# Seven-product stage: the low parts of the first weight sum on VectorE, and pads that put the tiles on one place modulo 256 bytes

## The chip, the cores and the metric

The kernel runs on one core of a Trainium2 chip. The metric is the device time of one execution in microseconds; the median of several executions stands for a kernel. TensorE (PE in the profile; PEld is its weight load) multiplies, VectorE (DVE), ScalarE (ACT) and GpSimd (POOL) do the rest, and the queue of SyncE (SP) issues nearly all loads and stores.

## The reference

One decoder layer on x of 1024 tokens by 1024 channels in float32. Cut to what matters:

```python
h = rms_norm(x, norm_mix_pre)
z = h @ w_in                                   # 1024 x 7424
z_pool, z_q, z_rwkv, z_gate = split(z)
y_pool = pool_branch(z_pool, ...) @ w_proj_pool
y_mem  = mem_attention(z_q, mem_n, w_mem_kv) @ w_proj_mem
y_rwkv = rwkv_branch(...) @ w_proj_rwkv        # a recurrence over the tokens
merged = gates[0] * y_pool + gates[1] * y_rwkv + gates[2] * y_mem
x = x + rms_norm(merged @ w_o, norm_mix_post)
h = rms_norm(x, norm_ffn_pre)
u_gate, u_val = split(causal_dwconv(h @ w_ffn_up, conv_w, conv_b))   # 1024 x 5632
x = x + rms_norm((gelu(u_gate) * u_val) @ w_ffn_down, norm_ffn_post)
```

## The kernel before

All gemms multiply float32 as three products of shorter numbers. A number is split into a high part (a copy into the type float32r, by ScalarE) and a low part (the number minus its high part, a subtraction), and `mm3` (lines 167 to 169) issues three matmuls of 128 by 128 weights with 512 moving columns: high x high, high weights x low moving, low weights x high moving. In the profile these are the tile pairs psg<-hh,whi, psg<-hl,whi and psg<-hh,wlo.

The stages, in the order of time, with the moving tiles and the weights:

- the input projection, moving hh and hl, weights whi and wlo. The recurrence of the RWKV branch runs among its gemms (lines 528 to 709: short float32 matmuls on tiles such as HV, AR, BKN); 928 steps of `mm3`
- attention and pooling with their projections: moving oh, ol, ph and pl
- the merge (moving yh, yl) and the output projection (mgh, mgl)
- the first five pairs of blocks of the up projection (h2h, h2l), with weights whi and wlo
- the seven-product stage (`up_pair`, PSUM tiles psf): the other 17 pairs of blocks of the up projection. The two blocks of a pair, gate and value, are cut in halves a11, a12 and a21, a22 over the channels, and the pair is computed with seven products in place of eight (Strassen's scheme). The panels B11, B21, B22, T4 lie in h2h and h2l, T1 and T2 and T3 in tiles t. The weights of the products are, in this order: a11 with B11; the first sum a21 + a22 with T1; the second sum, first sum minus a11, with T2; a12 with B21; a11 - a21 with T3; the third sum, a12 minus second sum, with B22; a22 with T4. First and second sum are done by GpSimd (line 1012) in the same tile sm, the third by VectorE, also in sm. `parts` splits the weights: high parts by ScalarE (line 1026), low parts by GpSimd (line 1027), each in two halves of 128 x 256. A product is 4 steps of `mm3`, 12 matmuls; a pair is 84. ScalarE and VectorE take the products out of PSUM and combine them (lines 1056 to 1075: u, z), ScalarE begins the convolution (line 1043, d<-z,pv), VectorE adds its taps (line 1045)
- the down projection, also with seven products (PSUM tiles psd, moving f, weights u)

The order on each engine is set by the scheduler of the tile framework, which keeps the order of dependent instructions; the first sum of a pair is made about one pair ahead.

Weights of the seven products have six buffers in turn, `n = nwt[0] % 6`: for n < 2 a tile of the pool `ow`, otherwise two tiles of the pool `pmp`. These pools lie at different places. A place is here the first byte of a tile within a partition, modulo 256; all tiles that matter have rows of a multiple of 256 bytes. The built programs have these places:

| tiles | before | after |
| --- | --- | --- |
| hh, hl, h2h, h2l, yh, yl, mgl (moving) | 224 | 224 |
| whi, wlo, wraw, sm, the a of later pairs | 192 | 224 |
| mgh, oh, ol, ph, pl (moving) | 64 | 224 |
| T1 and T2 (moving) | 64 | 224 |
| T3 (moving) | 224 | 224 |
| weights of the seven products, pool ow | 64 | 224 |
| weights of the seven products, pool pmp | 224 | 224 |
| f and u of the down projection | 64 | 224 |
| tiles of the recurrence (HV, AR, BK, NT and others) | 64 | 224 |
| constants ones, ident, bonesr, cent | 192 | 192 |

Of the kernel before, what the change touches and what calls it, by code (L numbers as in the profile page):

```python
# [9 lines left out]
F32 = mybir.dt.float32  # L10
FR = mybir.dt.float32r
AF = mybir.ActivationFunctionType
ALU = mybir.AluOpType
# [4 lines left out]
P = 128  # L18
# [26 lines left out]
def trunk_kernel(ctx: ExitStack, tc: tile.TileContext, xT, memT, pvec, w_in, w_kv, w_upd, w_upg,  # L45
                 w_pool, w_ppool, w_pmem, w_prwkv, w_o, w_fup, w_fdn, out):
    nc = tc.nc
    V, A, G, PE, SP = nc.vector, nc.scalar, nc.gpsimd, nc.tensor, nc.sync

    const = ctx.enter_context(tc.tile_pool(name="const", bufs=1))  # L50
    wp = ctx.enter_context(tc.tile_pool(name="wp", bufs=1))
# [53 lines left out]
                        base=-1, channel_multiplier=-1)  # L105
    G.memset(smask, 1.0)
    G.memset(smask.rearrange("p (c s) -> p c s", s=C)[:, :, 0:1], 0.0)
    eps = const.tile([P, 3], F32, name="eps")
    for j, e in enumerate((NORM_EPS, L2_EPS, LNX_EPS)):
        G.memset(eps[:, j:j + 1], e)  # L110
# [112 lines left out]
    for k in range(KC):  # L223
        tag = ("X01", "X11", "HV", "HV")[k // 2]
# [76 lines left out]

    def shifted(m, dst):

        zc = wp.tile([P, 1], F32, name="zc", tag="zc", bufs=4)

        def evac(t0, ps):
            d = dst[:, t0:t0 + 512]
            A.activation(d, ps, AF.Identity, scale=omu[:, m:m + 1])
            if t0 == 0:
                V.tensor_copy(zc, ps[:, 511:512])  # L310
            else:
                V.scalar_tensor_tensor(d[:, 0:1], zc, col("mu", m), d[:, 0:1], op0=ALU.mult,
                                       op1=ALU.add)
            V.scalar_tensor_tensor(d[:, 1:512], ps[:, 0:511], col("mu", m), d[:, 1:512],  # L314
                                   op0=ALU.mult, op1=ALU.add)
        return evac
# [532 lines left out]
    for hd in range(4):  # L849
        for t0, _ in HALVES:  # L850
            s = slice(t0, t0 + 512)
            q = as_.tile([P, 512], F32, name="q", tag="q", bufs=2)
            SP.dma_start(q, d_zq[hd][:, s])
            qh = as_.tile([P, 512], FR, name="qh", tag="qh")
            ql = as_.tile([P, 512], FR, name="ql", tag="ql")
            split(q, qh, ql, V)
            po = pss.tile([P, 512], F32, name="po", tag="s")
            for u in range(2):
                ps = psg.tile([P, 2, 256], F32, name="psco", tag="g0")
                for tt in range(2):  # L860
                    ts_ = slice((2 * u + tt) * P, (2 * u + tt + 1) * P)
                    mm3(ps[:, tt], (qh[:, ts_], ql[:, ts_]), (kh[:, hd], kl[:, hd]), True, True)
                mx = as_.tile([P, 8], F32, name="mxs", tag="mxs", bufs=2)
                V.reduce_max(mx[:, 0:2], ps, axis=AX.X)
                V.tensor_scalar(mx[:, 2:4], mx[:, 0:2], -SC, None, op0=ALU.mult)
                pr = as_.tile([P, 2, 256], F32, name="prb", tag="prb", bufs=2)
                for tt in range(2):
                    act(pr[:, tt], ps[:, tt], AF.Exp, bias=mx[:, 2 + tt:3 + tt], scale=SC,
                        accum_out=mx[:, 4 + tt:5 + tt])
                V.reciprocal(mx[:, 6:8], mx[:, 4:6])  # L870
                V.tensor_tensor(pr, pr, mx[:, 6:8].unsqueeze(2).broadcast_to([P, 2, 256]), op=ALU.mult)
                pt = (psc if u else psk).tile([P, 2, 2, P], F32, name="ptr", tag="c" if u else "k")
                for tt in range(2):
                    for m in range(2):
                        PE.transpose(pt[:, m, tt], pr[:, tt, m * P:(m + 1) * P], ident)
                pth = as_.tile([P, 2, 256], FR, name="pth", tag="pth", bufs=2)
                ptl = as_.tile([P, 2, 256], FR, name="ptl", tag="ptl")
                split(pt.rearrange("p m t s -> p m (t s)"), pth, ptl, V)
                for m in range(2):
                    mm3(po[:, u * 256:(u + 1) * 256], (vh[:, hd, m], vl[:, hd, m]), (pth[:, m], ptl[:, m]),  # L880
                        m == 0, m == 1)
            split(po, oh[hd][:, s], ol[hd][:, s], V)
        pool_products(hd)
        if hd < 2:
            pool_sums(hd + 2)
        for j, ev in fill[2 * hd:2 * hd + 2]:
            in_block(j, ev, 1)
# [109 lines left out]
    def up_pair(i):  # L997
        c = i % 2

        def load(nm, tag, j, k0):  # L1000
            if i == EARLY:
                t = ow.tile([P, 4, P], F32, name=nm, tag="xt" if tag == "whi" else "ss", bufs=2)
                SP.dma_start(t, w_fup[j][:, k0:k0 + 4])
                return [t[:, :2], t[:, 2:]]
            t = [wp.tile([P, 2, P], F32, name=nm, tag=f"{tag}{c}", bufs=4) for _ in range(2)]
            for u in range(2):
                SP.dma_start(t[u], w_fup[j][:, k0 + 2 * u:k0 + 2 * u + 2])
            return t

        def both(eng, out_, a, b, op):  # L1010
            for u in range(2):
                eng.tensor_tensor(out_[u], a[u], b[u], op=op)  # L1012

        def parts(src):

            n = nwt[0] % 6
            nwt[0] += 1
            if n < 2:
                w = ow.tile([P, 2, 4, P], FR, name="wt", tag=f"q{n}")
                w = [w[:, 0], w[:, 1]]  # L1020
            else:
                w = [pmp.tile([P, 4, P], FR, name=f"wt{e}", tag=f"n{8 + (n + 1) % 4 + 4 * e}")
                     for e in range(2)]
            for u in range(2):
                us = slice(2 * u, 2 * u + 2)
                A.copy(w[0][:, us], src[u])  # L1026
                last_low[0] = G.tensor_tensor(w[1][:, us], src[u], w[0][:, us].bitcast(F32), op=ALU.subtract).ins  # L1027
            return w

        nb = [0]  # L1030

        def prod(src, panel):
            w = parts(src)
            pool, tag = ((psg, "g0"), (psg, "g1"), (pss, "s"), (psk, "k"), (psg, "g0"), (psg, "g1"),
                         (pss, "s"))[nb[0]]
            nb[0] += 1
            ps = pool.tile([P, 512], F32, name="psf", tag=tag)
            for k in range(4):
                mm3(ps, (w[0][:, k], w[1][:, k]), panel(k), k == 0, k == 3)
            return ps  # L1040

        def convolved(z, d, j):
            A.activation(d, z, AF.Identity, scale=col("cw2", j), bias=col("cb", j))  # L1043
            for n, cw in ((1, "cw1"), (2, "cw0")):
                V.scalar_tensor_tensor(d[:, n:], z[:, :T - n], col(cw, j), d[:, n:], op0=ALU.mult,  # L1045
                                       op1=ALU.add)

        a11 = load("a11", "whi", i, 0)
        a21 = load("a21", "wlo", NF + i, 0)
        a22 = load("a22", "wlo", NF + i, 4)  # L1050
        a12 = load("a12", "whi", i, 4)
        sm = [wp.tile([P, 2, P], F32, name="sm", tag=f"wraw{c}", bufs=3) for _ in range(2)]
        z1, z2 = (ow1.tile([P, T], F32, name=f"z{e}", tag=f"q{4 + 2 * e + c}") for e in range(2))
        c11, c12, c21, c22 = z1[:, :512], z1[:, 512:], z2[:, :512], z2[:, 512:]
        u2 = ow.tile([P, 512], F32, name="u2", tag="xt", bufs=2)
        A.copy(c11, prod(a11, B11))
        both(G, sm, a21, a22, ALU.add)
        A.copy(c22, prod(sm, T1))
        both(G, sm, sm, a11, ALU.subtract)
        V.tensor_tensor(u2, c11, prod(sm, T2), op=ALU.add)  # L1060
        V.tensor_tensor(c22, c22, u2, op=ALU.add)
        V.tensor_tensor(c11, c11, prod(a12, B21), op=ALU.add)
        both(V, a21, a11, a21, ALU.subtract)
        p7 = prod(a21, T3)
        third = V.tensor_tensor(c21, u2, p7, op=ALU.add).ins
        if i == NF - 1:
            down.extend(down_loads())
            down.append(third)
        both(V, sm, a12, sm, ALU.subtract)
        V.tensor_tensor(c12, c22, prod(sm, B22), op=ALU.add)  # L1070
        last_sum[0] = V.tensor_tensor(c22, c22, p7, op=ALU.add).ins
        d1, d2 = (ow.tile([P, T], F32, name=f"d{e}", tag=f"q{2 + e}") for e in range(2))
        convolved(z1, d1, i)
        act(d1, d1, AF.Gelu_apprx_tanh)
        V.tensor_tensor(c21, c21, prod(a22, T4), op=ALU.add)
        convolved(z2, d2, NF + i)
        V.tensor_tensor(d1, d1, d2, op=ALU.mult)
        (G if i == NF - 1 else SP).dma_start(d_f[i], d1)
# [530 lines left out]
```

## Time and profile before

| | us |
| --- | --- |
| median of 3 executions | 2084.89 (2083.38 to 2085.0) |
| profiled execution | 2084.65 |
| its span, first to last instruction | 2082.7 |
| PE busy | 2026.5 |
| DVE busy | 1358.2 |
| ACT busy | 1070.6 |
| POOL busy | 810.8 |

The profile shows one execution. "Busy" is the time in which an engine worked on an instruction; matmuls are pipelined and overlap, and their ends are modelled, so the interval between the starts of two matmuls says more than the duration of one. A row of the view in order of time gives start and duration in us, engine, line, operation, tiles (out<-in), shape and, in brackets, how long the engine was idle before and who ended that. A row of the view of waits gives who waited for whom, the total in us, the times and the longest.

### The profile page before, as it was taken

The page shows a single profiled execution, that of the slowest core. Times are in us where ns is not written, and L with a number is a line of the kernel's source. Part 1 is how long each engine was busy: PE and PEld are TensorE (multiplying, and loading weights), DVE is VectorE, ACT ScalarE, POOL GpSimd, SP SyncE. Part 2 cuts the span into 40 slices and gives each one's busy share as a digit, 9 for nine tenths or more (in the row PEclk, how much of TensorE's full clock was granted, in tenths as well). Part 3 has the DMA queues.
Part 4 walks back from the last instruction along what each step waited for, and adds up shares of the span by engine and source line. Part 5 has one row for each costly group of instructions (what it writes and reads, how often), then busy time and mean ns, then how long its engine had stood idle before and what let it go on. Part 6 is the DMA issues. An engine that isn't in the chain of part 4 may idle for free.

```text
span 2082.7 us, 34125 instructions
## 1 busy us (share of the span) xinstructions
PE 2026.5 (97%) x12246; PEld 1559.1 (75%) x12246; DVE 1358.2 (65%) x2167; ACT 1070.6 (51%) x2252; POOL 810.8 (39%) x917
## 2 busy tenths in 40 slices
PE   8999999999999999999999999998999999999997
PEld 5777767776778667876878878776778877777886
DVE  6567437664667357833795452769877777777798
ACT  7585348623772368434566243545443444444644
POOL 5521213121222121212122355565578888842341
PEclk9999999999999999999999999999999999999999
DMA  4312211120212021213526443634222222169766
GB/s 155 129 41 74 67 51 67 67 82 22 87 61 89 30 92 44 86 55 120 172 84 223 129 134 107 220 102 151 94 88 83 82 78 76 61 185 273 168 178 152
DMA packets 176713, 221.83 MB, mean 107 GB/s; under 512 B 16544, under 2 KB 128288, under 8 KB 176544
## 3 DMA queue, kind: packets, MB, share of 16 engines
q1 hardware_dynamic: 163616, 204.44, 30.2%
q0 software_dynamic: 11856, 14.16, 4.2%
q8 instruction: 97, 1.59, 0.3%
q10 hardware_dynamic: 1072, 1.05, 0.1%
q14 instruction: 72, 0.59, 0.1%
HBM read 170.30 MB, written 49.28 MB: 105 GB/s over the span
## 4 chain that ended last, share of the span: by engine, by line
PE 36%; DVE 5%; DMA 4%; POOL 3%; issue 2%; ACT 2%; SPq 1%; POOLq 0%; ACTq 0%; DVEq 0%
PE psg L167 6%; PE psg L169 6%; PE psg L168 6%; PE psf L169 3%; PE psf L167 3%; PE psf L168 3%; POOL wt L1027 2%; PE psd L168 2%; PE psd L169 2%; PE psd L167 2%; DMA R<-d_f 1%; POOL sm L1012 1%; DMA a<-in_w_fup 1%; ACT d L1043 1%; DMA fw<-in_w_fdn 1%
## 5 line engine op out<-in xcount | busy, mean ns | idle before, releaser
L131 POOL TENSOR_TENSOR wlo<-wraw,whi 128x256 fp32r<-128x256 f32 x472 | 410.4, 878 | 951.7 <-ACT whi L128 760.2
L167 PE MATMUL psg<-hh,whi 128*128 128x512 f32 x928 | 383.6, 413 | 2.5 <-DVE kv L314 2.5
L169 PE MATMUL psg<-hh,wlo 128*128 128x512 f32 x928 | 379.8, 409 | 0.1
L168 PE MATMUL psg<-hl,whi 128*128 128x512 f32 x928 | 378.8, 408 | 0.0
L128 ACT CAST whi<-wraw 128x256 fp32r<-128x256 f32 x472 | 182.7, 403 | 227.9 <-PE psg L168 122.1
L167 PEld LDWEIGHTS psg<-hh,whi 128*128 128x128 f32 x928 | 174.6, 188 | 46.5 <-DVE kv L314 3.8
L169 PEld LDWEIGHTS psg<-hh,wlo 128*128 128x128 f32 x928 | 174.3, 188 | 45.9 <-POOL wlo L131 5.1
L168 PEld LDWEIGHTS psg<-hl,whi 128*128 128x128 f32 x928 | 174.7, 188 | 42.9 <-issue 3.6
L1027 POOL TENSOR_TENSOR wt<-a,wt 128x256 fp32r<-128x256 f32 x136 | 133.8, 1012 | 30.8 <-ACT wt L1026 30.8
L167 PE MATMUL psd<-f,u 128*128 128x512 f32 x292 | 115.0, 394 | 5.7 <-ACT f L1347 3.4
L168 PE MATMUL psd<-f,u 128*128 128x512 f32 x292 | 115.0, 394 | 1.0 <-DVE f L1351 1.0
L169 PE MATMUL psd<-f,u 128*128 128x512 f32 x292 | 114.3, 393 | 0.4 <-DVE u L1351 0.4
L1027 POOL TENSOR_TENSOR wt<-sm,wt 128x256 fp32r<-128x256 f32 x102 | 106.8, 1067 | 14.6 <-ACT wt L1026 14.6
L169 PE MATMUL psf<-h2h,wt 128*128 128x512 f32 x272 | 108.0, 397 | 0.4 <-POOL wt L1027 0.3
L168 PE MATMUL psf<-h2l,wt 128*128 128x512 f32 x272 | 107.0, 393 | 0.0
L167 PE MATMUL psf<-h2h,wt 128*128 128x512 f32 x272 | 106.8, 393 | 0.0
L1026 ACT CAST wt<-sm 128x256 fp32r<-128x256 f32 x102 | 37.9, 404 | 128.2 <-POOL sm L1012 124.2
L1045 DVE SCALAR_TENSOR_TENSOR d<-z,pv,d 128x1023 f32<-128x1023 f32 x68 | 91.6, 1347 | 12.0 <-ACT d L1043 9.5
L169 PE MATMUL psf<-t,wt 128*128 128x512 f32 x204 | 81.3, 399 | 1.9 <-POOL wt L1027 1.9
L168 PE MATMUL psf<-t,wt 128*128 128x512 f32 x204 | 80.3, 394 | 0.0
L167 PE MATMUL psf<-t,wt 128*128 128x512 f32 x204 | 80.2, 393 | 0.0
L685 DVE TENSOR_TENSOR HV<-ph,Hd 64x128 f32<-64x128 f32 x112 | 32.3, 289 | 71.8 <-PE ph L639 47.7
(422 smaller groups left out, 4751.3 us busy)
## 6 DMA issues: line engine op xcount, KB each, us to landing
wraw<-in_w_in SPq DMA_DIRECT2D x240, 128.0 KB, 2.3
a<-in_w_fup SPq DMA_DIRECT2D x128, 128.0 KB, 2.4
d_zg<-st SPq DMA_DIRECT2D x48, 256.0 KB, 2.7
wraw<-in_w_fup SPq DMA_DIRECT2D x80, 128.0 KB, 2.4
fw<-in_w_fdn SPq DMA_DIRECT2D x33, 256.0 KB, 4.5
fraw<-d_f SPq DMA_DIRECT2D x33, 256.0 KB, 5.2
wraw<-in_w_prwkv SPq DMA_DIRECT2D x64, 128.0 KB, 2.4
wraw<-in_w_o SPq DMA_DIRECT2D x64, 128.0 KB, 2.5
```

What stands on the lines that cost most here:

```text
L128: last_whi[0] = A.copy(hi, src).ins
L131: (V if lo_on_dve[0] else G).tensor_tensor(lo, src, hi.bitcast(F32), op=ALU.subtract)
L167: first = PE.matmul(ps, wh, xh, start=start, stop=False)
L168: PE.matmul(ps, wh, xl, start=False, stop=False)
L169: last_mm[0] = PE.matmul(ps, wl, xh, start=False, stop=stop).ins
L685: ready = V.tensor_tensor(HV[q, :, c + 1, e], ph[q], Hd[q], op=ALU.add).ins
L1012: eng.tensor_tensor(out_[u], a[u], b[u], op=op)
L1026: A.copy(w[0][:, us], src[u])
L1027: last_low[0] = G.tensor_tensor(w[1][:, us], src[u], w[0][:, us].bitcast(F32), op=ALU.subtract).ins
L1043: A.activation(d, z, AF.Identity, scale=col("cw2", j), bias=col("cb", j))
L1045: V.scalar_tensor_tensor(d[:, n:], z[:, :T - n], col(cw, j), d[:, n:], op0=ALU.mult, op1=ALU.add)
```

## The change

Two things are done. The pads: a tile of 8 columns that nobody uses in the pool `const`, eight buffers of one column in place of four for zc, and 32 columns in place of 8 for mxs. Allocation is in steps of 32 bytes, so these move the tiles allocated behind them (table above). And `parts` takes the engine of the low parts as an argument; the product with T1 passes VectorE, so the low parts of the first sum (2 per pair, 34 in all) are done there. `last_low` keeps the last low part on GpSimd.

```diff
     G.memset(smask.rearrange("p (c s) -> p c s", s=C)[:, :, 0:1], 0.0)
+    const.tile([P, 8], F32, name="cpad")
...
-        zc = wp.tile([P, 1], F32, name="zc", tag="zc", bufs=4)
+        zc = wp.tile([P, 1], F32, name="zc", tag="zc", bufs=8)
...
-                mx = as_.tile([P, 8], F32, name="mxs", tag="mxs", bufs=2)
+                mx = as_.tile([P, 32], F32, name="mxs", tag="mxs", bufs=2)
...
-        def parts(src):
+        def parts(src, eng):
...
                 A.copy(w[0][:, us], src[u])
-                last_low[0] = G.tensor_tensor(w[1][:, us], src[u], w[0][:, us].bitcast(F32), op=ALU.subtract).ins
+                low = eng.tensor_tensor(w[1][:, us], src[u], w[0][:, us].bitcast(F32), op=ALU.subtract)
+                if eng is G:
+                    last_low[0] = low.ins
             return w
...
-        def prod(src, panel):
-            w = parts(src)
+        def prod(src, panel, eng=G):
+            w = parts(src, eng)
...
-        A.copy(c22, prod(sm, T1))
+        A.copy(c22, prod(sm, T1, V))
```

Where the low parts stand now is seen in the middle of the seven-product stage. Lines are up to three later in the changed kernel (1012 becomes 1013, 1027 becomes 1028, 1060 becomes 1063), and the numbers of tiles are one higher. GpSimd before: the first sum of one pair (sm_16855), then the low parts T1 of the pair before it (wt1_16703<-sm_16675), its second sum in the same tile, and its low parts T2:

```order
L1012 TENSOR_TENSOR sm_16855<-a21_16843,a22_16847 128x256
L1012 TENSOR_TENSOR sm_16856<-a21_16844,a22_16848 128x256
L1027 TENSOR_TENSOR wt1_16703<-sm_16675,wt0_16702 128x256
L1027 TENSOR_TENSOR wt1_16703<-sm_16676,wt0_16702 128x256
L1012 TENSOR_TENSOR sm_16675<-sm_16675,a11_16659 128x256
L1012 TENSOR_TENSOR sm_16676<-sm_16676,a11_16660 128x256
L1027 TENSOR_TENSOR wt1_16725<-sm_16675,wt0_16724 128x256
L1027 TENSOR_TENSOR wt1_16725<-sm_16676,wt0_16724 128x256
```

GpSimd at the same place now:

```order
L1013 TENSOR_TENSOR sm_16856<-a21_16844,a22_16848 128x256
L1013 TENSOR_TENSOR sm_16857<-a21_16845,a22_16849 128x256
L1013 TENSOR_TENSOR sm_16676<-sm_16676,a11_16660 128x256
L1013 TENSOR_TENSOR sm_16677<-sm_16677,a11_16661 128x256
L1028 TENSOR_TENSOR wt1_16726<-sm_16676,wt0_16725 128x256
L1028 TENSOR_TENSOR wt1_16726<-sm_16677,wt0_16725 128x256
```

The low parts T1 are gone, and the second sum, which overwrites the first, follows the first sum of the next pair at once; it has to wait for the low parts on the other engine. VectorE before, at the same place: the subtraction a11 - a21 of the later pair, u and z of an earlier one, the third sum, z:

```order
L1012 TENSOR_TENSOR a21_16843<-a11_16839,a21_16843 128x256
L1012 TENSOR_TENSOR a21_16844<-a11_16840,a21_16844 128x256
L1060 TENSOR_TENSOR u2_16500<-z0_16498,psf_16550 128x512
L1061 TENSOR_TENSOR z1_16499<-z1_16499,u2_16500 128x512
L1062 TENSOR_TENSOR z0_16498<-z0_16498,psf_16571 128x512
L1012 TENSOR_TENSOR sm_16675<-a12_16671,sm_16675 128x256
L1012 TENSOR_TENSOR sm_16676<-a12_16672,sm_16676 128x256
L1065 TENSOR_TENSOR z1_16499<-u2_16500,psf_16593 128x512
L1070 TENSOR_TENSOR z0_16498<-z1_16499,psf_16614 128x512
```

VectorE now:

```order
L1013 TENSOR_TENSOR a21_16844<-a11_16840,a21_16844 128x256
L1013 TENSOR_TENSOR a21_16845<-a11_16841,a21_16845 128x256
L1063 TENSOR_TENSOR u2_16501<-z0_16499,psf_16551 128x512
L1028 TENSOR_TENSOR wt1_16704<-sm_16676,wt0_16703 128x256
L1064 TENSOR_TENSOR z1_16500<-z1_16500,u2_16501 128x512
L1028 TENSOR_TENSOR wt1_16704<-sm_16677,wt0_16703 128x256
L1065 TENSOR_TENSOR z0_16499<-z0_16499,psf_16572 128x512
L1013 TENSOR_TENSOR sm_16676<-a12_16672,sm_16676 128x256
L1013 TENSOR_TENSOR sm_16677<-a12_16673,sm_16677 128x256
L1068 TENSOR_TENSOR z1_16500<-u2_16501,psf_16594 128x512
L1073 TENSOR_TENSOR z0_16499<-z1_16500,psf_16615 128x512
```

The two low parts stand behind u and behind the first z; the rest of VectorE's order is the same, and TensorE's order is unchanged.

## Prediction

> **What bounds the kernel now.** I read the page first, then who waited for whom, then the matmuls in order of time, and last the three other engines in one stretch of the seven-product stage.
>
> ```profile
> span 2082.7 us, 34125 instructions
> PE 2026.5 (97%) x12246; PEld 1559.1 (75%) x12246; DVE 1358.2 (65%) x2167; ACT 1070.6 (51%) x2252; POOL 810.8 (39%) x917
> ...
> PE psn L1096 <- DVE s L1091: 8.3, 1, 8.3
> PEld psf L169 <- POOL wt L1027: 10.6, 22, 0.8
> ```
>
> TensorE is busy for 97% of the span, and its longest single wait is 8.3 us. So time can come from two things: from a shorter interval between matmuls that follow each other without a wait, and from small waits such as the 22 on GpSimd's low parts in the seven-product stage. The column "us" of a matmul is modelled; the interval is the difference of two starts. I took the starts 24 matmuls apart in three stages without waits: the input projection, the output projection, the down projection.
>
> ```profile
> 424.83 0.40 PE L169 MATMUL psg<-hh,wlo 128*128 128x512 f32 x1
> ...
> 430.43 0.40 PE L169 MATMUL psg<-hh,wlo 128*128 128x512 f32 x1
> ...
> 1359.64 0.39 PE L167 MATMUL psg<-mgh,whi 128*128 128x512 f32 x1
> ...
> 1365.18 0.39 PE L167 MATMUL psg<-mgh,whi 128*128 128x512 f32 x1
> ...
> 1959.73 0.39 PE L168 MATMUL psd<-f,u 128*128 128x512 f32 x1
> ...
> 1965.17 0.39 PE L168 MATMUL psd<-f,u 128*128 128x512 f32 x1
> ```
>
> 24 matmuls of the same shape take 5.60 us (233.3 ns each) with hh at place 224 and the weights at 192; 5.54 us (230.8 ns) with mgh at 64 and the weights at 192; and 5.44 us (226.7 ns) with f and u both at 64. Three stages could differ for other reasons. The seven-product stage has the test inside itself, since its weight tiles rotate over two places while the panels stay. These rows are the first matmuls of products of 12 matmuls each:
>
> ```profile
> 1606.16 0.39 PE L167 MATMUL psf<-h2h,wt 128*128 128x512 f32 x1
> ...
> 1608.88 0.40 PE L167 MATMUL psf<-t,wt 128*128 128x512 f32 x1
> ...
> 1625.30 0.39 PE L167 MATMUL psf<-h2h,wt 128*128 128x512 f32 x1
> ...
> 1628.11 0.39 PE L167 MATMUL psf<-t,wt 128*128 128x512 f32 x1
> ...
> 1630.84 0.39 PE L167 MATMUL psf<-t,wt 128*128 128x512 f32 x1
> ...
> 1633.64 0.39 PE L167 MATMUL psf<-h2h,wt 128*128 128x512 f32 x1
> ```
>
> B11 from 1606.16 has panel and weights at 224: 2.72 us. B11 one pair later, from 1625.30, has the same panel at 224 and its weights at 64: 2.81 us. T1 from 1628.11 has both at 64: 2.73 us; T2 from 1630.84 has the panel at 64 and the weights at 224: 2.80 us. Equal places are fast whichever place it is, unequal ones cost some 7 ns a matmul. I take the place modulo 256 as the cause, and 226.7 ns as the price with equal places. By the Trainium skill, page "SBUF — State Buffer", section "Who interferes with whom", TensorE never waits for anyone and only the port pair of VectorE and GpSimd is contended; it speaks against any effect of places on TensorE, and the four products above differ from it by 0.07 to 0.09 us each.
>
> **The pads.** They put moving tiles and weights of all gemms on 224. How many matmuls that are:
>
> ```profile
> L168 PE MATMUL psg<-hl,whi x928: 388/396/795, 7.4 to 1101.5; 128*128 128x512 f32 x186
> ...
> L168 PE MATMUL psf<-h2l,wt x272: 387/393/401, 1508.7 to 1844.8; 128*128 128x512 f32 x136
> ...
> L168 PE MATMUL psg<-h2l,whi x160: 388/396/628, 1380.7 to 1507.8; 128*128 128x512 f32 x160
> ...
> L168 PE MATMUL psg<-yl,whi x128: 392/395/398, 1196.0 to 1334.6; 128*128 128x512 f32 x128
> ...
> L168 PE MATMUL psg<-mgl,whi x128: 389/392/796, 1240.8 to 1380.0; 128*128 128x512 f32 x128
> ```
>
> Line 168 is one of the three matmuls of each step, so each count stands for three times as many.
> - hh and hl: 2784 x 6.6 ns = 18.4 us if each gains. Many stand among the short products of the recurrence, where the interval isn't 0.23 us:
>
> ```profile
> 252.03 0.39 PE L167 MATMUL psg<-hh,whi 128*128 128x512 f32 x1
> 252.35 0.45 PE L639 MATMUL ph<-HV,BKN 128*64 128x64 f32 x8
> ```
>
> Here it is 0.32 us, and nothing in the trace says that this one shrinks. I take two thirds, 12.2 us; ends 9 and 18.4.
> - h2h and h2l: 480 x 6.6 = 3.2 us. yh and yl, at the places of hh: 384 x 6.6 = 2.5 us. mgh and mgl: 384 x (230.8 - 226.7) = 1.6 us. The attention and pooling projections, 64 against 192 like mgh, are 2 x 8 blocks x 2 halves x 4 steps x 3 = 384: 1.6 us.
> - The down projection is at equal places already: 0. The seven-product stage is counted by itself below.
>
> Together 21.1 us. The extra buffers of zc and the wider mxs add no instruction: 0. The operands of copies, sums and activations change their places too. Those engines end few of TensorE's waits outside the seven-product stage (the 8.3 us above are the longest), so I count 0.
>
> **The low parts of the first sum.** 34 subtractions leave GpSimd and join VectorE. The stage is a loop of GpSimd, VectorE and ScalarE, which TensorE runs ahead of and then has to wait for. One round of it, the three engines one after the other (GpSimd, VectorE, ScalarE):
>
> ```profile
> 1664.78 0.73 POOL L1012 TENSOR_TENSOR sm<-a,a 128x256 f32<-128x256 f32 x1
> 1666.10 0.73 POOL L1012 TENSOR_TENSOR sm<-a,a 128x256 f32<-128x256 f32 x1 [0.58 <-DMA a<-in_w_fup]
> 1666.79 1.62 POOL L1027 TENSOR_TENSOR wt<-sm,wt 128x256 fp32r<-128x256 f32 x2
> 1668.36 1.90 POOL L1012 TENSOR_TENSOR sm<-sm,a 128x256 f32<-128x256 f32 x2
> 1670.21 1.42 POOL L1027 TENSOR_TENSOR wt<-sm,wt 128x256 fp32r<-128x256 f32 x2
> ...
> 1675.65 3.34 POOL L1027 TENSOR_TENSOR wt<-sm,wt 128x256 fp32r<-128x256 f32 x2 [0.84 <-ACT wt L1026]
> 1680.40 4.66 POOL L1027 TENSOR_TENSOR wt<-a,wt 128x256 fp32r<-128x256 f32 x4 [1.41 <-ACT wt L1026]
> 1685.02 0.74 POOL L1012 TENSOR_TENSOR sm<-a,a 128x256 f32<-128x256 f32 x1
> ...
> 1665.55 0.42 DVE L1012 TENSOR_TENSOR a<-a,a 128x256 f32<-128x256 f32 x1 [2.71 <-POOL sm L1012]
> 1666.87 0.94 DVE L1012 TENSOR_TENSOR a<-a,a 128x256 f32<-128x256 f32 x1 [0.89 <-POOL sm L1012]
> 1667.73 0.68 DVE L1060 TENSOR_TENSOR u<-z,psf 128x512 f32<-128x512 f32 x1
> 1668.51 1.15 DVE L1061 TENSOR_TENSOR z<-z,u 128x512 f32<-128x512 f32 x1
> ...
> 1670.98 1.82 DVE L1012 TENSOR_TENSOR sm<-a,sm 128x256 f32<-128x256 f32 x2 [0.72 <-POOL wt L1027]
> ...
> 1673.32 0.68 DVE L1070 TENSOR_TENSOR z<-z,psf 128x512 f32<-128x512 f32 x1
> ...
> 1674.03 1.25 ACT L1043 ACTIVATE d<-z,pv 128x1024 f32<-128x1024 f32 x1 [2.11 <-DVE z L1070]
> ```
>
> First sum to first sum is 20.24 us, while TensorE needs 19.14 for a pair (1606.16 to 1625.30). The loop is this: second half of the first sum (1666.10); low parts T1, second sum, low parts T2 on GpSimd; VectorE's third sum, which waited 0.72 us for GpSimd (1670.98); z (1673.32); ScalarE's convolution (1674.03); its casts, for which GpSimd waits 0.84 and 1.41 us; the last low parts, and so the load that the next first sum waits for. The stage confirms it: 16 rounds of 20.24 and a last pair of 19.1 make 342.9 us; it takes 336.7 (1508.4 to 1845.1: the quoted row's ends, out by the two matmuls around them); TensorE's lead, eaten up over the first seven pairs, is the other 6.2.
>
> Now the second sum has to wait until VectorE has read the first. By durations: the first sum's second half ends at 2.05 us of the round, as now. VectorE then does its subtraction, 2.09 to 2.52 (0.42 as at 1665.55, with GpSimd now idle there), u until 3.12 (0.68), and the first low part until 3.47. GpSimd's second sum may start at 3.5; it started at 3.58. Its first half is held up by z (0.67 to 1.15 us), ends at 4.7, and holds up VectorE's second low part until some 5.0 (0.95 as in the blocked rows). The second half of the second sum ends at 5.8 where it ended at 5.5 (1668.36 + 1.90 - 1664.78), and everything behind it, T2, third sum, z, convolution, moves by 0.3. So taking 1.6 us off GpSimd doesn't shorten the round: its work there lies beside VectorE's, and the 0.72 us that VectorE waited become 0.8 us of work and the rest a later start. Ends: 0.72 us shorter, if both low parts fit where VectorE waits now and nothing blocks; 1.2 longer, if both take 0.95 and only 0.72 of it is covered (2 x 0.95 - 0.72). I take 0.3, from the chain above.
>
> The stage: 16 x 20.54 + 19.1 - 6.2 = 341.5, so 4.8 us longer, and the faster matmuls gain nothing here, as TensorE only uses up its lead earlier.
>
> **The sum.** 21.1 - 4.8 = 16.3 us. The profiled execution took 2084.65 us (span 2082.7 and 1.95 around it), 0.24 under the median of 2084.89. 2084.65 - 16.3 = 2068.4.
>
> **The rivals.**
> - The loop gets shorter, not longer. At 0.72 us less it is 19.5, and less still where GpSimd's free time also shortens VectorE's blocked operations (0.94 to 0.42); TensorE's lead then lasts and it sets the stage: 17 x 84 x 226.7 ns = 323.7, and 0.6 of waits: 12.4 us less than 336.7. Time 2084.65 - 21.1 - 12.4 = 2051. For it: GpSimd is the busiest of the helpers in the stage. Against: the waits of 0.84 and 1.41 us on ScalarE, which it doesn't touch.
> - The loop is 1.2 us longer: 16 x 1.2 = 19.2, time 2082.8. VectorE's 0.94 and 1.82 show how often its operations are blocked; against it, GpSimd is idle when the first low part runs.
> - Places don't set the interval, and the four products differ by something else that rotates with the tiles. This is the side that ends slower: the pads bring 0, the move still costs 4.8, time 2089.5. It decides when an aligned matmul gains under some 0.2 ns. Against it: 2.72, 2.81, 2.73, 2.80. By the page named above it would come to this.
> - The gain is partial, because other traffic at one common place takes some of it back: half of 21.1 leaves 2078.9. The down projection has its matmul operands at 64 and loads tiles at 224, so no stage shows all at one place.
>
> **How the numbers follow.** My forecast (2062 to 2074) 0.47; the short loop 0.22; the long loop 0.13; a partial gain 0.10; no effect of places 0.08. Predicted is the first, 2068.4. The range from 2048 to 2080 leaves out half of the long loop (0.06), all of the last case (0.08) and the low edge of the short loop (0.04). 0.2% of the time, about what a measurement of this kernel can tell from no change, is 4.2 us: faster is below 2080.7, which holds the first two, nearly all partial gains and two thirds of the long loop, 0.87; the rest of the long loop and a part of the last case, 0.07, is no change; 0.06 is slower.
>
> **What would show it.** In the new profile 24 matmuls on hh should take 5.44 us, B11 2.72 us in every pair, and the down projection what it takes now. On GpSimd first sum to first sum should be about 20.5, with second sums that wait for VectorE, and VectorE's third sum should still wait for T2's low parts. The prediction is wrong if intervals on hh stay at 233 ns, or if the round falls under 19.2 us.

## The result, and the profile after

The changed kernel takes 2079.43 us (median of 22 runs, 2076.27 to 2084.65), the kernel before beside it 2083.70 (22 runs). The ratio is 0.9981, with an interval of 0.9975 to 0.9987: about 4 us are gained, where 16 were forecast. The profiled executions differ by 6.1 us of span (2082.7 and 2076.6).

The page of the changed kernel, and two rows of TensorE's waits in its stretch from 1350 to 1845 us (us in total, times, longest):

```profile
span 2076.6 us, 34082 instructions
...
PE 2010.1 (97%) x12246; PEld 1553.0 (75%) x12246; DVE 1360.1 (65%) x2201; ACT 1071.3 (52%) x2252; POOL 785.4 (38%) x883
...
PE psn L1099 <- DVE s L1094: 9.3, 1, 9.3
PE psf L170 <- DVE wt L1028: 5.0, 11, 0.9
```

TensorE is busy for 16.4 us less, yet the span is only 6.1 us shorter. The wait at the norm is 1.0 us longer than before (8.3), and in the seven-product stage TensorE now waits for VectorE's low parts. Matmuls in order of time, at the places of the prediction's rows:

```profile
248.78 0.40 PE L168 MATMUL psg<-hh,whi 128*128 128x512 f32 x1
249.11 0.28 PE L640 MATMUL ph<-HV,BKN 128*64 128x64 f32 x2
...
421.23 0.39 PE L170 MATMUL psg<-hh,wlo 128*128 128x512 f32 x1
...
426.67 0.39 PE L170 MATMUL psg<-hh,wlo 128*128 128x512 f32 x1
...
1953.69 0.39 PE L169 MATMUL psd<-f,u 128*128 128x512 f32 x1
...
1959.13 0.39 PE L169 MATMUL psd<-f,u 128*128 128x512 f32 x1
```

24 matmuls on hh now take 5.44 us instead of 5.60, the down projection takes 5.44 as before, and between recurrence products the interval is 0.33 us (it was 0.32). So equal places do what was forecast in the long run of hh, and in this place of the recurrence nothing.

One round of the seven-product stage, from first sum to first sum; GpSimd, VectorE, and the one wait of TensorE in it:

```profile
1676.93 1.80 POOL L1013 TENSOR_TENSOR sm<-a,a 128x256 f32<-128x256 f32 x2 [0.40 <-DMA a<-in_w_fup]
1680.20 1.12 POOL L1013 TENSOR_TENSOR sm<-sm,a 128x256 f32<-128x256 f32 x1 [1.47 <-DVE wt L1028]
1681.68 0.74 POOL L1013 TENSOR_TENSOR sm<-sm,a 128x256 f32<-128x256 f32 x1 [0.36 <-DVE wt L1028]
...
1697.19 0.74 POOL L1013 TENSOR_TENSOR sm<-a,a 128x256 f32<-128x256 f32 x1
...
1677.70 0.43 DVE L1013 TENSOR_TENSOR a<-a,a 128x256 f32<-128x256 f32 x1 [3.16 <-POOL sm L1013]
1678.76 0.43 DVE L1013 TENSOR_TENSOR a<-a,a 128x256 f32<-128x256 f32 x1 [0.63 <-POOL sm L1013]
1679.11 0.68 DVE L1063 TENSOR_TENSOR u<-z,psf 128x512 f32<-128x512 f32 x1
1679.70 0.42 DVE L1028 TENSOR_TENSOR wt<-sm,wt 128x256 fp32r<-128x256 f32 x1
...
1680.64 0.96 DVE L1028 TENSOR_TENSOR wt<-sm,wt 128x256 fp32r<-128x256 f32 x1
...
1683.15 1.83 DVE L1013 TENSOR_TENSOR sm<-a,sm 128x256 f32<-128x256 f32 x2 [0.95 <-POOL wt L1028]
...
1680.17 0.50 PE L170 MATMUL psf<-t,wt 128*128 128x512 f32 x1 [0.60 <-DVE wt L1028]
```

The round is 20.26 us here (1676.93 to 1697.19), one of the shorter ones; by TensorE's starts, pairs six to sixteen take 20.38 to 20.96 us, mean 20.56. The second sum waits 1.47 and 0.36 us for VectorE's low parts, and VectorE's third sum waits 0.95 us for GpSimd, all as the chain of the prediction had it. From the end of the first sum to the end of the second it is 3.69 us (1678.73 to 1682.42), where it was 3.43 before (1666.83 to 1670.26): these are the 0.3 us of the forecast. Ahead of all that VectorE stands idle for 3.16 us, with the subtraction a11 - a21 of the next pair at its head, which waits for the first sum of that pair.

### The profile page after: what moved, and what is told of

It reads as the page before. It is cut to its first block, busy times and chain, and to the rows that moved or that the text cites. A ratio compares the mean times of both kernels' runs of the same rounds, so it can differ in the third digit from the quotient of the medians.

```text
span 2076.6 us, 34082 instructions
## 1 busy us (share of the span) xinstructions
PE 2010.1 (97%) x12246; PEld 1553.0 (75%) x12246; DVE 1360.1 (65%) x2201; ACT 1071.3 (52%) x2252; POOL 785.4 (38%) x883
## 5 line engine op out<-in xcount | busy, mean ns | idle before, releaser
L1028 POOL TENSOR_TENSOR wt<-a,wt 128x256 fp32r<-128x256 f32 x136 | 133.9, 1012 | 29.4 <-ACT wt L1027 29.4
L1028 POOL TENSOR_TENSOR wt<-sm,wt 128x256 fp32r<-128x256 f32 x68 | 79.3, 1186 | 14.6 <-ACT wt L1027 14.6
```

The costliest lines, as they stand in the source:

```text
L1028: low = eng.tensor_tensor(w[1][:, us], src[u], w[0][:, us].bitcast(F32), op=ALU.subtract)
```

## The experiments

Starts and intervals of TensorE that no fence shows are worked out from the traces' matmul starts. "Lead" is how much earlier the same matmul starts in one trace than in another.

**Each half alone.** e1 has the pads and leaves the low parts on GpSimd; e2 has the low parts on VectorE and no pads:

```diff
 e1 (against the changed kernel)
-        A.copy(c22, prod(sm, T1, V))
+        A.copy(c22, prod(sm, T1))
 e2 (against the kernel before; parts and prod as in the change)
-        A.copy(c22, prod(sm, T1))
+        A.copy(c22, prod(sm, T1, V))
```

> The changed kernel with the low parts of the first sum on GpSimd again; the pads stay. Theory A (places shorten the interval in long runs of matmuls only, and the round of the seven-product stage is set by the chain GpSimd, VectorE, ScalarE, which the move of the low parts made longer): the lead of 11.2 us at the start of the seven-product stage stays as in the changed kernel, the stage takes 336.7 us as before the change (first sum to first sum 20.2 us), total 11 us less than before, about 2072.5. Rival B (the round got longer because all tiles now lie at one place, not because of the move): the stage takes 342 us here too, about 2078. Rival C (every aligned matmul gains 6.6 ns): 21 us less than before, 2063.

> The kernel before with the low parts of the first sum on VectorE; no pads. Theory A: round of 20.5 us, the seven-product stage 5 us longer, total 2089. Rival B: the round stays at 20.2 us, total as before, 2084.

Measured on one chip, where the kernel before takes 2078.94: e1 2073.15 (ratio 0.9971, 0.9959 to 0.9983), 5.8 us gained, where 11 were expected; e2 2082.09 (1.0015, 1.0006 to 1.0024), 3.2 us lost, where 5 were expected. The two have the same order up to the seven-product stage, so their traces show what the pads bring there. Lead of e1 over e2, in us, beside the forecast added up to the same place:

| up to | forecast | e1 over e2 | changed over before |
| --- | --- | --- | --- |
| last matmul on hh (1101.7 us before) | 12.2 | 8.1 | 7.4 |
| end of attention and pooling, first matmul of the merge (1195.8) | 13.8 | 10.2 | 9.5 |
| start of the seven products (1508.4) | 21.1 | 6.3 | 11.2 |

Each column compares two single executions, and the middle one is generous to the pads: the profiled execution of e1 was its fastest (2069.48 against the median of 2073.15), that of e2 was above its median (2083.38). Over all traces the first two rows stand firm. The last matmul on hh starts at 1093.1 to 1096.1 us in the seven traces with hh and its weights on equal places (the changed kernel, e1, e4, and e9 to e12 below) and at 1101.2 to 1101.9 in before, e2 and e3; the first matmul of the merge at 1185.1 to 1188.1 in those seven and at 1195.8 and 1195.3 in before and e2.

The third row depends on the execution. Busy time by stretch (sum, then the engines, the granted clock, DMA), of before and then of e2, which has the same places:

```profile
1240.00:1300.00 60.00, 57.42 (x242) 45.81 (x241) 16.25 (x22) 24.51 (x57) 33.44 (x44) 0.97 0.35 106
...
1240.00:1300.00 60.00, 60.00 (x261) 48.45 (x260) 17.32 (x24) 24.32 (x57) 34.03 (x44) 1.00 0.34 110
```

In this execution of before TensorE waited 2.6 us for a copy of the merge and ran at a mean granted clock of 0.97, and did 242 matmuls where e2 did 261. The rows behind that wait show a second cost of it: the next matmuls start 0.43 us apart instead of 0.23, as long as the granted clock (the column behind the counts) is 0.50.

```profile
1248.20 0.80 PE L167 MATMUL psg<-mgh,whi 128*128 128x512 f32 x1 [2.58 <-ACT mgh L121]
...
1249.94 0.63 PE L167 MATMUL psg<-mgh,whi 128*128 128x512 f32 x1
1250.37 0.63 PE L168 MATMUL psg<-mgl,whi 128*128 128x512 f32 x1
...
1248.00:1251.00 3.00, 2.80 (x6) 1.98 (x7) 1.38 (x2) 1.06 (x4) 2.30 (x3) 0.50 0.13 32
```

From the first matmul of the merge to the first of the seven products it is 312.6 us in before and 305.4 in e2, and 306.4 to 310.9 in the five traces that have all pads and the additions of squares on VectorE (the changed kernel, e1, e4, e10, e12). So of the 7.3 us that the pads were to gain there, these traces show none clear of the scatter. TensorE's waits from 1170 to 1512 us, first all of e2, then the longest of e1:

```profile
PE psn L1098 <- DVE s L1093: 7.4, 1, 7.4
PE psg L169 <- DVE wlo L131: 0.4, 1, 0.4
...
PE psn L1099 <- DVE s L1094: 9.2, 1, 9.2
PE psg L170 <- DVE wlo L132: 2.4, 2, 2.0
PE psg L168 <- ACT mgh L122: 2.3, 1, 2.3
```

7.8 us of waits become 13.9 (14.7 with three of 0.2 to 0.3); in the other four of the five traces they are 13.2 to 14.6. Between these two executions the 3.9 us lost (10.2 to 6.3) divide so: the waits grow by 6.9 us, the matmuls at half the clock behind them cost some 2.0 more (3.7 against 1.7), and everything else is 5.0 faster. What the faster matmuls gain, TensorE spends waiting for sums, weights and the merge's copies. Before had 12.2 us of waits itself, so how much of the growth is the pads' doing, one pair of traces can't tell.

The seven-product stage in e1 and e2, from the first matmul on h2l to the last:

```profile
L169 PE MATMUL psf<-h2l,wt x272: 387/389/397, 1494.6 to 1829.5; 128*128 128x512 f32 x136
...
L168 PE MATMUL psf<-h2l,wt x272: 388/393/400, 1500.9 to 1843.4; 128*128 128x512 f32 x136
```

334.9 us with the pads alone, 342.5 with the low parts alone; it was 336.1 before (1508.7 to 1844.8). In e1 pairs two to five take 19.04 us, while TensorE's lead lasts, and pairs from the seventh on 20.1 to 20.2, in e2 20.4 to 20.5 with two of 20.9 and 21.2: the move costs the loop some 0.3 to 0.4 us a round, and the pads give the loop nothing (in before it is 20.1 to 20.3).

**Pads of the same kind, places unequal.** e3 has every pad, but the first is 16 columns wide, so that the weights of the gemms come to 0 while hh, hl, yh, yl, mgl and the panels h2h, h2l stay at 224 (attention, pooling and mgh come to 0 with their weights); low parts on GpSimd:

```diff
-    const.tile([P, 8], F32, name="cpad")
+    const.tile([P, 16], F32, name="cpad")
...
-        A.copy(c22, prod(sm, T1, V))
+        A.copy(c22, prod(sm, T1))
```

> Pads only, but the unused constant is 16 columns in place of 8, so the tiles on the left side lie at place 0 and those on the right side (hh, hl, h2h, h2l, yh, yl, mgl and a part of the weights of the seven products) at 224. Theory A (what counts is that moving tile and weights have the same place): 24 matmuls on hh take 5.60 us as before the change; mgh with its weights is equal and takes 5.44; total 1 to 3 us less than before, about 2082. Rival D (pads as such, or the wider spacing of buffers, bring the gain): as with the other pads, about 2072.5.

```profile
424.65 0.40 PE L170 MATMUL psg<-hh,wlo 128*128 128x512 f32 x1
...
430.25 0.40 PE L170 MATMUL psg<-hh,wlo 128*128 128x512 f32 x1
```

2077.78 us, ratio 0.9995 (0.9986 to 1.0004), no change clear of the noise, and 24 matmuls on hh take 5.60 us, as before the change. It is the equality of the two places that shortens the interval, not another layout as such. By the Trainium skill, page "SBUF — State Buffer", section "Who interferes with whom", TensorE's moving operand and its weight load have ports of their own and are independent of each other. This case's runs show more than that: 233 ns with unequal and 227 ns with equal places, whatever the reason.

**The run without a break.** In the changed kernel the intervals between hh and hl matmuls fall after a pause (an interval of 0.30 us or more between two of them): 233.6, 233.1, 230.9, 229.9, 229.1, 228.3, 227.0 ns for the first seven and 226.7 from the thirteenth on (168 intervals at the first place, 1223 from the thirteenth on). Before, they go from 230.1 to 233.3. To test that, one short float32 matmul, its result unread, is put into the first half's merge and output projection, behind every step of three matmuls (e5, e6) or behind every fourth step (e7, e8), with equal places (e5, e7; else as e1) and with the places of before (e6, e8; else as the kernel before). Each of the four was executed once, so only intervals inside their traces are compared:

```diff
             m = mm3(ps, ws[k], rhs(k), k == 0, k == n - 1)
...
+            if brk[0] is not None:          # e7, e8: and k % 4 == 3
+                PE.matmul(brk[0][:, 0:64], ident, ones[:, 0:64], start=True, stop=True)
```

> Equal places as in the pads alone, and after every step of three matmuls of the first half's merge and output projection one short float32 matmul (128x64, result unread). Theory (equal places pay only after a run of six to eight matmuls without a break): the intervals inside the steps stay at 230 to 235 ns, as after the breaks of the changed kernel (233.5, 233.1, 230.6), and not 226.7. Rival (every matmul with equal places is 6 ns shorter, wherever it stands): 227 ns inside the steps.

> The same breaks, places as in the kernel before. Theory of the run: intervals inside the steps as with equal places within 2 ns, so the time from the first matmul of merge to the last of the output projection's first half differs by under 0.6 us from the run with equal places. Rival: 5.5 ns each, so some 112 x 2 x 5.5 ns = 1.2 us or more longer, and 232.3 ns inside the steps against 227.

> Equal places, one short matmul after every 12. Theory of the run: the interval falls along each run of twelve, from some 233 ns at its start to 227 from the seventh on; mean over the first eleven intervals 229 to 230. Rival: 227 at each position.

> Places as before, one short matmul after every 12. Both theories: 230 to 235 ns at every position with no fall along the run, mean some 232 to 233. If here too the interval falls to 227 from the seventh on, then it is the run and not the places that makes the difference, and both are wrong.

Starts of steps three steps apart, e5 and then e6:

```profile
1200.35 0.48 PE L168 MATMUL psg<-yh,whi 128*128 128x512 f32 x1
...
1203.10 0.47 PE L168 MATMUL psg<-yh,whi 128*128 128x512 f32 x1
...
1206.75 0.48 PE L167 MATMUL psg<-yh,whi 128*128 128x512 f32 x1
...
1209.51 0.48 PE L167 MATMUL psg<-yh,whi 128*128 128x512 f32 x1
```

Mean intervals in ns, start to start:

| | equal places | as before |
| --- | --- | --- |
| steps of three: second matmul to third, third to the break (111 each) | 230.1, 233.3 (e5) | 229.4, 232.6 (e6) |
| the same traces where no break was put, yh and yl later than twelfth in a run (166) | 226.7 (e5) | 233.3 (e6) |
| twelve and a break: intervals of the second to the eleventh matmul (26 to 28 each) | 234.5, 233.7, 235.2, 224.9, 231.0, 234.5, 228.3, 231.9, 230.5, 226.5 (e7) | 228.5, 232.1, 233.6, 230.3, 232.3, 233.0, 232.1, 230.5, 233.5, 231.6 (e8) |

With a break after every step, three steps take 2.75 and 2.76 us, and equal places bring nothing; in the same two runs, unbroken, they bring 6.6 ns. With a break after twelve the mean is 231.1 against 231.8: a tenth of the gain, less than the half that I expected. The rival of a fixed gain for each matmul is out. How long the run must be isn't settled: 227.0 ns is reached at the seventh interval behind a pause on hh, and not steadily within the eleven of e7. Why the start of a run is slow is open too.

**Holding a subtraction back.** e4 is the changed kernel with one order added: the subtraction a11 - a21 of the next pair comes behind the second low part of T1 on VectorE (line 1069):

```diff
+                else:
+                    t1_low[1] = low.ins
...
-        both(V, a21, a11, a21, ALU.subtract)
+        for u in range(2):
+            d = V.tensor_tensor(a21[u], a11[u], a21[u], op=ALU.subtract)
+            if t1_low[0] is not None:
+                later(d, t1_low[0])
+        t1_low[0] = t1_low[1]
```

> The changed kernel, with the subtractions a11 - a21 of the next pair held back until VectorE has done the low parts T1, so that these fall into the time in which VectorE waits for GpSimd's first sum. Theory A: the chain from the second half of the first sum to the third sum loses GpSimd's two low parts (1.6 us) and gets no VectorE work in their place; the round falls under TensorE's 19.04 us a pair, the stage takes about 325 us, 17 less than in the changed kernel, total about 2062. Rival E (VectorE is full in this stage, so it doesn't matter where its two operations stand): stage 340 to 345 us, total 2077 to 2082.

2053.31 us beside the 2078.94 of before, ratio 0.9875 (0.9862 to 0.9889), 25.6 us gained, more than I expected. VectorE's waits from 1490 to 1850 us, the largest of the changed kernel and then the row of e4 for the same subtraction; then a round of e4 on GpSimd and on VectorE, and its stage:

```profile
DVE a L1013 <- POOL sm L1013: 55.0, 30, 3.4
...
DVE a L1069 <- POOL sm L1013: 8.8, 14, 0.6
...
1659.92 1.61 POOL L1013 TENSOR_TENSOR sm<-a,a 128x256 f32<-128x256 f32 x2
1661.48 1.80 POOL L1013 TENSOR_TENSOR sm<-sm,a 128x256 f32<-128x256 f32 x2
...
1657.20 0.67 DVE L1065 TENSOR_TENSOR u<-z,psf 128x512 f32<-128x512 f32 x1
1657.79 0.41 DVE L1028 TENSOR_TENSOR wt<-sm,wt 128x256 fp32r<-128x256 f32 x1
...
1659.28 0.95 DVE L1028 TENSOR_TENSOR wt<-sm,wt 128x256 fp32r<-128x256 f32 x1
1660.86 1.82 DVE L1069 TENSOR_TENSOR a<-a,a 128x256 f32<-128x256 f32 x2 [0.63 <-POOL sm L1013]
...
L169 PE MATMUL psf<-h2l,wt x272: 389/389/397, 1493.6 to 1817.3; 128*128 128x512 f32 x136
```

55.0 us of VectorE's idle time fall to 8.8. The low parts now begin ahead of the first sum of the next pair (1657.79 and 1659.28 against 1659.92), not behind it, and the second sum follows that at once. Pairs two to sixteen take 19.04 us each, the stage 323.7: TensorE sets it. Before, the pairs that TensorE set (two to six) took 19.14 to 19.51 us, so the pads should pay here too; the same order without pads, or with the low parts left on GpSimd, was not run.

**The wait at the norm.** e9 is e4's kernel with seven additions of squares moved from VectorE to GpSimd; e10 is e4's kernel once more beside it:

```diff
-            sumsq(s2, o[k], k == 0, V)
+            sumsq(s2, o[k], k == 0, G if n else V)
```

> e4's kernel with seven additions of squares of the second half's residual moved from VectorE to GpSimd. Theory (between the merge and the seven-product stage the pads gain nothing because VectorE sets the end there): VectorE is freed of 7 x 0.9 = 6 us ahead of the norm, TensorE's wait at the norm falls from 9.2 us to 4 to 7, and the time is 2 to 5 us under that of e4's kernel beside it. Rival (the wait at the norm is set by the chain of loads, residuals and squares, or GpSimd's additions come later than VectorE's): wait and time within 1 us of e4's, or longer by what the low parts of the weights, queued behind the additions on GpSimd, make TensorE wait.

> e4's kernel once more, beside e9 on the same chip. As before: 0.9875 of the kernel before (0.986 to 0.989), and TensorE's lead in the seven-product stage growing by 14 to 16 us over the kernel before.

Beside 2082.98 of before: e10 2057.22 (0.9880, 0.9863 to 0.9896), so e4's gain holds on another chip, though TensorE's lead over the kernel before grows by 11.2 us in the stage (336.6 to 325.3, first start to last), not by the 14 to 16 that I expected; e9 2063.22 (0.9905, 0.9889 to 0.9921), 6.0 us slower than e10, with some 4.8 to either side. TensorE's waits from 1170 to 1512 us, first of e10 and then of e9, and e9's group of the moved additions:

```profile
PE psn L1105 <- DVE s L1100: 9.4, 1, 9.4
...
PE psg L170 <- POOL wlo L132: 0.9, 2, 0.5
...
PE psn L1105 <- POOL s L1100: 5.9, 1, 5.9
PE psg L170 <- POOL wlo L132: 5.3, 6, 1.6
...
L1100 POOL TENSOR_TENSOR s<-s,sq 128x512 f32<-128x512 f32 x7 | 10.5, 1503 | 0.6 <-ACT sq L1099 0.3 <-DMA a<-in_w_fup 0.2
```

The wait at the norm falls from 9.4 to 5.9 us, as my theory had it, but the weights' low parts queue behind additions of 1.5 us on GpSimd, and their waits grow from 0.9 to 5.3. My theory's sum was wrong: VectorE is not the only engine that is full there.

**The panels of the up projection on unequal places again.** e11 is e1 with a pad behind the panels h2h and h2l, which come to 192 (weights 224): 480 matmuls of the first up projection and 816 of the seven products lose their equal places, and every order stays. e12 is e1 once more:

```diff
+    hf.tile([P, 8], F32, name="hpad")
     uf = [hf.tile([P, KC, 512], FR, name="uf", tag=tag) for tag in ("h2l0", "h2l1")]
```

> e1's kernel with the panels h2h and h2l moved by 32 bytes, so that 480 matmuls of the first up projection and 816 of the seven products have moving tile and weights on unequal places again, 1296 in all; every order is as in e1's kernel. Theory (there the helper engines set the end, and equal places only make TensorE wait longer): within 1.5 us of e1's kernel beside it. Rival (each of these is worth 6.6 ns, as the prediction had it for the 480): 3.2 us longer if only the 480 count, 8.6 us if all do.

> e1's kernel once more, beside e11 on the same chip. As before: 0.9971 of the kernel before (0.996 to 0.998).

Beside 2079.24 of before: e11 2072.73 (0.9965, 0.9952 to 0.9979), e12 2073.06 (0.9967, 0.9955 to 0.9980). The stages, e11 first, with its wait at the norm:

```profile
PE psn L1099 <- DVE s L1094: 8.2, 1, 8.2
...
L168 PE MATMUL psf<-h2h,wt x272: 392/396/403, 1499.8 to 1835.3; 128*128 128x512 f32 x136
L168 PE MATMUL psg<-h2h,whi x160: 392/396/1416, 1371.0 to 1499.1; 128*128 128x512 f32 x160
...
L168 PE MATMUL psf<-h2h,wt x272: 387/389/402, 1497.7 to 1833.1; 128*128 128x512 f32 x136
L168 PE MATMUL psg<-h2h,whi x160: 387/389/1415, 1370.5 to 1497.0; 128*128 128x512 f32 x160
```

The seven-product stage is 335.5 and 335.4 us: pairs take 19.4 us instead of 19.04 while the lead lasts, and both run at 20.1 to 20.2 after. The first up projection takes 128.1 against 126.5; that is half of the 3.2 us of its 480 matmuls, but the same stage takes 128.9 us in e1 and 125.3 in e2 (first start to the start of the seven products), so a single execution doesn't tell. What becomes of a gain shows at the norm: the same 146 matmuls ahead of it take 34.2 us in e11 (1371.0 to 1405.2) and 33.3 in e12 (1370.5 to 1403.8), and the wait that follows is 8.2 us in e11 and 9.3 in e12, so that TensorE goes on at 1413.8 and 1413.5: the 0.9 us are lost in the wait. In the time the difference is -0.3 us, with some 3.8 to either side (the two half-widths, 2.8 and 2.6, in quadrature). 8.6 us, the price of all 1296, is excluded; 3.2 is near the edge and isn't.

## Why the prediction was wrong

- **The interval with equal places: right.** 5.60 became 5.44 us for 24 matmuls on hh, and with places unequal again (e3) it is 5.60.
- **hh and hl, 12.2 us: the first step that failed.** The traces show 8.1 (e1 over e2) and 7.4. The mechanism was right; the size was wrong. I cut 18.4 by a third for the recurrence on the row of 0.32 us, without counting. Counted, 1424 of the 2784 stand ninth or later in a run without a break, and 1424 x 6.6 ns = 9.4; that is also what their intervals gain from e2 to e1. The 273 intervals at places three to seven of a run gain 1.2 us together, the 410 at the first two places lose 0.6 (e5 against e6 shows the same for runs of three), 33 intervals with a wait in them lose 2.0, and all others together bring nothing: 8.1.
- **Attention and pooling, 1.6: right, a little low** (10.2 - 8.1 and 9.5 - 7.4, both 2.1).
- **Merge, output projection, first up projection, 7.3: the second step that failed, and the larger one.** They brought nothing that the traces show: -3.9 in one pair of traces, +1.7 in the other, and 306.4 to 310.9 us with pads against 305.4 and 312.6 without. I counted every faster matmul there in full. Of TensorE's waits I noted only that the other engines end few of them outside the seven-product stage, and took that for a sign of slack. The wait of 8.3 us at the norm said otherwise: TensorE stood there until VectorE's sum had come, and matmuls that end earlier ahead of such a wait lengthen it (8.2 us in e11, 9.3 in e12). Part of the gain goes to matmuls at half the clock behind the waits. e11 takes the equal places of the up projection away, and no change shows in the time, with 3.8 us to either side. Which of the helpers holds the stretch is not settled: e9 relieved VectorE and loaded GpSimd, and lost.
- **Down projection, 0: right;** 5.44 us before and after.
- **The low parts, round 0.3 longer, stage +4.8: right.** The stage went from 336.1 to 341.1 (1497.5 to 1838.6 by its row on h2l), +5.0, and e2 over before shows 342.5, +6.4 (1.4 of it in its first pair, 21.45 us against 20.09). That the faster matmuls gain nothing in the stage was right too: even in e1, without the move, it is only 1.2 us shorter than before, though its first pairs take 19.04 us instead of 19.14 to 19.51.

```profile
L169 PE MATMUL psf<-h2l,wt x272: 387/389/397, 1497.5 to 1838.6; 128*128 128x512 f32 x136
```

So of 21.1 us the pads kept 5.8 to 6.2 (e1, e12), the low parts took 3.2 (e2), and the sum, some 3, fits the 4.3 measured (2.7 to 5.2 by the interval). The case nearest to what came was the rival of the partial gain, at 2078.9, to which I gave 0.10. That it came so near is luck: its reason, traffic at one common place, isn't what the runs show.

One thing I read past: the rival of the shorter loop needed VectorE's low parts to fit where VectorE waits. VectorE's row of 2.71 us idle at the subtraction a11 - a21 stood in my fence. I looked for cover in the 0.72 us at the third sum, and not at why VectorE stood still while the low parts were ready to be made. With that subtraction behind them (e4), the stage of that rival came out: 324.2 us from first start to last in e4 and 325.3 in e10, where the rival had 324.3 with its waits.

## What to carry to other kernels

A faster inner instruction is worth its count only where TensorE runs without breaks and nobody else sets the next point in time: count the matmuls that stand in long runs, and look for the first long wait behind each stage, since what is gained ahead of it can be given back there. Where an operation moves to another engine, look at what stands at the head of that engine's queue and waits: here the move lost 3 us by itself, and one reordering behind it brought more than 20.

## What the runs showed of the hardware

- 128x512 float32r matmuls follow each other every 226.7 ns when moving tile and weights begin at the same place modulo 256 bytes (224 and 64 were seen), and every 230 to 233 ns at the unequal places seen (224 with 192, 224 with 0, 64 with 192; before, e1, e3). I knew that from the trace before, but not that the lower figure comes only some way into an unbroken run.
- After a break the first intervals are the same for equal and unequal places (230.1 and 229.4 ns, e5 and e6), and twelve matmuls between breaks aren't enough for the gain (231.1 and 231.8 ns, e7 and e8).
- After a wait TensorE can run slower for a while: around the wait at the norm the granted clock is 0.50 for 6.8 to 10.2 us, the end of the wait included, in all ten traces without breaks, and the matmuls there start 427 ns apart (before, 1425.70 to 1428.26). Behind waits of 2.0 to 2.6 us the lower clock came in some cases (before, 2.6 us at the merge; e1, 2.0 us at 1487.6) and not in others (e1, 2.3 us at 1235.8; e4, 2.1 us at 1238.1).
- GpSimd's addition of 128x512 took 1503 ns (mean of seven, e9) while VectorE's work lay beside it; VectorE's additions in the same place took 676 to 1222 ns (six, in e4). By the Trainium skill, page "SBUF — State Buffer", section "Who interferes with whom", a VectorE instruction with two inputs in SBUF contends with a GpSimd instruction that reads SBUF. The changed kernel agrees: VectorE's low part takes 0.42 us with GpSimd idle (1679.70) and 0.96 beside its subtraction (1680.64).
